# Seven-product weight sets for the merge gates, with a Mamba-2 (SSD) mixer cut into half groups beside them

## The chip, the core and the metric

The kernel runs on one core of a Trainium2 chip. TensorE (PE in the profile; PEld is its weight load) multiplies, VectorE (DVE), ScalarE (ACT) and GpSimd (POOL) do the elementwise work, and SyncE (SP) issues nearly all transfers. The metric is the time of one execution in device microseconds (us). Three runs of the kernel before took 1894.10, 1894.57 and 1894.77 us; the median is 1894.57 us.

## The reference

One decoder layer on 1024 tokens of width 1024, all in float32:

```
h  = RMSNorm(x);  P = h @ W_in                     # one projection, about 9250 columns
a  = RetNet retention (4 heads)                    -> 1024
b  = Mamba-2 SSD (16 heads of 64, 2 groups, state 128, chunks of 128 tokens) -> 1024
c  = gated linear attention (4 heads)              -> 1024
x  = x + (sig(g_a)*a + sig(g_b)*b + sig(g_c)*c) @ W_out
x  = x + relu(RMSNorm(x) @ W_up)^2 @ W_down;       final RMSNorm
```

The SSD part, for each chunk and head, with `a_cs` the running sum of the log decay inside the chunk:

```
l_mat  = exp(where(causal, a_cs[l] - a_cs[m], -inf))
y_diag = ((C B^T) * l_mat) @ xs                    # xs = x * dt
y_off  = (C @ state) * exp(a_cs)
state  = exp(a_cs[-1]) * state + B^T @ (xs * exp(a_cs[-1] - a_cs))
```

The three merge gates `sig(g + bias)` are 3072 columns of `P`: twelve sets of 256 columns.

## The kernel before

Float32 operands are split into a high and a low part by `split` (a cast on ACT, L156, and a subtraction on DVE, L157), and each product is three matmuls, high by high, high by low, low by high (`acc3`, L164). The input projection runs over 34 weight sets of 256 output columns. `projections` (L390 on) runs them one after the other: it fetches the raw weights two sets ahead, and `prep` makes the parts of the next set while `run_set` multiplies the current one.

A set has one of two forms. A "plain" set is four output tiles of 24 matmuls of 512 columns each, so 96. A "block" set takes the 2 by 2 blocks of weights and activations and forms the four output tiles from seven block products of 12 matmuls each (Strassen-Winograd), so 84; for that `prep` makes four more sums on DVE (L327 to L334) and the sums of the activations lie ready in `ht`. In a block set ACT copies the first product out of PSUM (L367), DVE adds it twice (`plus`, L361), and three of the four output tiles need one more DVE addition in the emitter (for the gates L487) ahead of the activation (L488). A set yields after each product (7 steps for a block set) or each output tile (4 steps for a plain set), and `merge` lays the steps of a mixer between these steps. The recording layer then sets each engine's order; the engines work through it strictly in that order.

Of the twelve gate sets, the first four are block sets and the last eight plain. The order of the stages is: 20 block sets, beside the first of them the rotary and the decay computations and the causal convolutions; four block sets beside the retention mixers; two block sets beside the log decays of GLA (`log_decays`); then `ht` is given up and the plain sets run beside `ssd_mixer(0)` and `ssd_mixer(1)` (26 steps), then the row statistics (`ssd_rows`), then the last five steps beside the first loads of the branch products.

`ssd_mixer(g)` works on a group of eight heads, chunk by chunk. `stage_a` loads the chunk (`xin`, and `ab`, the decay sums broadcast to all partitions), turns x and B by TensorE transposes (L705, L707), forms C B^T (L708), the scaled x (`xs`, `xd`), a copy of B (`bt`, ACT, L717), `eb` = exp of the decays (ACT, L725), and the decay mask in `ab`: a minimum with the row's own decay on DVE (L726), an exp with the negated decay as bias on ACT, one per head (L728), and a product with the masked C B^T on DVE (L729). `stage_b` multiplies (L741, L746, L750), adds up `y` and stores it; a sum of squares per row follows by a matmul against ones (L772). The exp of the mixer and the sigmoid of the gates are in different activation tables, so an ACT_TABLE_LOAD stands at each change between them.

At the start, `v_unit` multiplies the first 256 value columns together with the 32 columns of the SSD step sizes and the GLA gate (`w_vdg`), whose weights come in two pieces of 1152 columns (L961).

Of the kernel before, what the change touches and what calls it, by code (L numbers as in the profile page):

```python
# [51 lines left out]
def _layout(inp):  # L52
# [3 lines left out]
    a["w_vdg"] = vdg.reshape(2, 4, P, 288).transpose(0, 2, 1, 3).reshape(2, P, 1152)  # L56
# [55 lines left out]
def block_kernel(ctx, tc, i, out):  # L112
# [101 lines left out]
    ssq = ac.tile([P, 2 * NT], F32, name="ssq")  # L214
# [5 lines left out]
    nacs = ac.tile([P, NT, SH], F32, name="nacs")  # L220
# [66 lines left out]
    def v_unit(c, hc, p, ws):  # L287
        width = (288, 256)[p]
        ps = pmm.tile([P, 512], F32, name="mm", tag="mm")
        pairs = []  # L290
        for k in range(KD):
            hi, lo = ws[k // 4]
            o = (k % 4) * width
            pairs.append((hc[k], (hi[:, o:o + width], lo[:, o:o + width])))
# [200 lines left out]
    def decays():  # L495
# [32 lines left out]
        V.tensor_scalar(out=nacs, in0=acs, scalar1=-1.0, scalar2=None, op0=ALU.mult)  # L528
# [159 lines left out]
    def ssd_mixer(g):  # L688
        R = SH // SG
        hs = slice(g * R, (g + 1) * R)  # L690
        st = {"s": None}
        live = {}
# [3 lines left out]

        def stage_a(c):
            xin = sp.tile([P, 10, P], F32, name="xin", bufs=3)
            nc.sync.dma_start(out=xin, in_=st_d[g][c])
            ab = sp.tile([P, R, P], F32, name="ab", bufs=2)  # L700
            r0 = c * SH + g * R
            nc.sync.dma_start(out=ab, in_=acs_d[r0:r0 + R, :].partition_broadcast(P))
# [6 lines left out]
            ptv = pt.rearrange("p (h d) -> p h d", h=R)  # L709
            xs = sp.tile([P, R, SP], F32, name="xs", tag="w2m", bufs=11)  # L710
            V.tensor_tensor(out=xs, in0=ptv, in1=hb(dt, c), op=ALU.mult)
            xd = bt = eb = None
            if c + 1 < NT:
                xd = sp.tile([P, R, SP], F32, name="xd", tag="w2m", bufs=11)
                V.tensor_tensor(out=xd, in0=ptv, in1=hb(dtd, c), op=ALU.mult)
                bt = sp.tile([P, P], F32, name="bt", bufs=2)
                S.copy(out=bt, in_=bc[:, 0:128])  # L717
            cbm = sp.tile([P, P], F32, name="cbm", bufs=2)
            V.tensor_tensor(out=cbm, in0=bc[:, 128:256], in1=tri, op=ALU.mult)
            if c > 0:  # L720
                eb = sp.tile([P, 4, P], F32, name="eb", tag="w2m", bufs=11)
# [10 lines left out]
        def stage_b(c):  # L732
            xin, ab, xs, xd, bt, eb = live.pop(c)
            state = st["s"]
            y = sp.tile([P, 4, P], F32, name="y", tag="w2m", bufs=11)
            G.tensor_tensor(out=y, in0=xin[:, 0:4, :],
                            in1=d_c[:, 4 * g:4 * g + 4].unsqueeze(2).broadcast_to([P, 4, P]), op=ALU.mult)
# [5 lines left out]
            if c > 0:  # L743
                yo = pmx.tile([P, 4, P], F32, name="mx", tag="mx")
                for k in range(4):
                    PE.matmul(out=yo[:, k, :], lhsT=state[:, 2 * k:2 * k + 2, :].rearrange("p h d -> p (h d)"),  # L746
                              rhs=xin[:, 5, :], start=True, stop=True)
            if c + 1 < NT:
                sp_ = pmx.tile([P, 512], F32, name="mx", tag="mx")
                PE.matmul(out=sp_, lhsT=bt, rhs=xd.rearrange("p h d -> p (h d)"), start=True, stop=True)  # L750
                new = sp.tile([P, R, SP], F32, name="sst", tag="sst", bufs=2)
                nf = new.rearrange("p h d -> p (h d)")
                if c == 0:
                    V.tensor_copy(out=nf, in_=sp_)
                else:
                    G.tensor_tensor(out=new, in0=state, in1=hb(cdec, c), op=ALU.mult)
                    V.tensor_tensor(out=nf, in0=nf, in1=sp_, op=ALU.add)
                st["s"] = new
            V.tensor_tensor(out=y, in0=yd, in1=y, op=ALU.add)
            if c > 0:  # L760
                V.tensor_tensor(out=eb, in0=yo, in1=eb, op=ALU.mult)
                V.tensor_tensor(out=y, in0=y, in1=eb, op=ALU.add)
            V.tensor_tensor(out=y, in0=y, in1=xin[:, 6:10, :], op=ALU.mult)
            nc.sync.dma_start(out=o_d[2 + g][c // 4][:, :, c % 4, :], in_=y)
            sq = sp.tile([P, 4, P], F32, name="ysq", tag="w2m", bufs=11)
            S.activation(out=sq, in_=y, func=AF.Square)
            G.tensor_tensor(out=sq[:, 0:2], in0=sq[:, 0:2], in1=sq[:, 2:4], op=ALU.add)
            G.tensor_tensor(out=sq[:, 0], in0=sq[:, 0], in1=sq[:, 1], op=ALU.add)

            def stat():  # L770
                ps = ptp.tile([P, 512], F32, name="tp", tag="tp")
                PE.matmul(out=ps[:, 0:1], lhsT=sq[:, 0], rhs=ones[:, 0:1], start=True, stop=True)  # L772
                V.tensor_copy(out=ssq[:, g * NT + c:g * NT + c + 1], in_=ps[:, 0:1])
            return stat

        pend = []
        stage_a(0)
# [10 lines left out]
        yield  # L788
# [3 lines left out]
    def ssd_rows():  # L792
        r = rstd(wk, ssq, SH // SG * SP, 2 * NT)
# [132 lines left out]
    for g in range(SG):  # L926
        n = SET_S + 5 * g
        ssd.append([(n, e_conv(g, [(8 + g, 4), (10 + g, 5)]))])
        for m in range(2):
            ssd[g].append((n + 1 + 2 * m, e_plain(st_d[g], 6 + 2 * m, AF.Silu)))  # L930
            ssd[g].append((n + 2 + 2 * m, e_conv(g, [(4 * g + 2 * m, 2 * m), (4 * g + 2 * m + 1, 2 * m + 1)])))
    for n, (slot, func) in enumerate(((0, None), (2, None), (6, AF.Silu), (8, AF.Silu), (10, None), (12, None))):
# [3 lines left out]
            gla[3], ssd[1][4], gla[4], gla[5]]  # L936
    jobs = [("block", *j) for j in jobs]
    jobs += [("block" if n < 4 else "plain", SET_M + n, e_gate(n // 4, 2 * (n % 4))) for n in range(12)]
# [20 lines left out]
    def v_raw(name, q, n):  # L959
# [409 lines left out]
```

## Time and profile before

| what | value |
|---|---|
| median of three runs | 1894.57 us |
| the profiled execution | 1895.59 us, its span 1893.8 us |
| granted TensorE clock over the span | 0.995 |
| PE busy | 1863.7 us, 98% |
| DVE busy | 1129.8 us, 60% |
| ACT busy | 817.6 us, 43% |
| POOL busy | 204.6 us, 11% |
| chain that ended last | PE 34%, of it the line of all split matmuls, L164, 34% |

The stretches of the span, by the lines that run in them: block sets alone from 285 to 484 us, the retention mixers from 484 to 566 us, the log decays from 587 us, the SSD mixers beside plain sets from 643 to 836 us, GLA beside the branch products from 880 to 1000 us, after that output projection and MLP. Busy times of a matmul group overlap their neighbours, so the pace of TensorE is read from the count of matmuls in a stretch, not from the mean time of one.

### The profile page before, as it was taken

The numbers are of one execution on the slowest core, as the hardware profiler recorded it, in microseconds if no ns is written. First come the engines' busy times: TensorE is split into PE (matmuls) and PEld (weight loads), VectorE is DVE, ScalarE is ACT, GpSimd is POOL, SyncE is SP. The second block draws the span as 40 slices with busy tenths as digits, with TensorE's granted clock in tenths as the row PEclk, the third lists the DMA queues.
The fourth block names the chain that finished last, engine by engine and source line by source line (L and its number), as shares of the span: only waits on it lengthen the run. The fifth ranks groups of instructions, "written<-read, shape, count | busy, mean of one in ns | idle before, by whom it ended". The sixth has DMA issues, their size and how long they took to land. (4 is left out here: it accounts for less than half of the span.)

```text
span 1893.8 us, 25031 instructions
## 1 busy us (share of the span) xinstructions
PE 1863.7 (98%) x9372; PEld 1540.5 (81%) x9372; DVE 1129.8 (60%) x1707; ACT 817.6 (43%) x1432; POOL 204.6 (11%) x219
## 2 busy tenths in 40 slices
PE   8999999999999999999999999999999999999998
PEld 8977778888887777787878889988888888888886
DVE  6867766667555486746687467575545434444444
ACT  7522333334455687845663123454544421112213
POOL 1011100000220132321231030000000000000003
PEclk9999999999999999999999999999999999999999
DMA  6434434332753665547468454532323363322322
GB/s 215 149 112 145 134 98 128 97 111 90 222 151 117 236 210 175 179 123 262 154 211 300 147 153 157 200 134 98 125 94 120 124 218 103 97 89 89 98 70 89
DMA packets 174329, 275.89 MB, mean 146 GB/s; under 512 B 12384, under 2 KB 113792, under 8 KB 167552
## 3 DMA queue, kind: packets, MB, share of 16 engines
q1 hardware_dynamic: 173632, 273.38, 44.8%
q8 instruction: 74, 1.21, 0.3%
q10 hardware_dynamic: 576, 0.92, 0.2%
q14 instruction: 47, 0.39, 0.1%
HBM read 191.33 MB, written 78.72 MB: 143 GB/s over the span
## 5 line engine op out<-in xcount | busy, mean ns | idle before, releaser
L156 ACT CAST whi<-raw 128x1024 fp32r<-128x1024 f32 (+1 forms) x223 | 233.8, 1050 | 514.2 <-PE mm L164 484.8
L157 DVE TENSOR_TENSOR wlo<-raw,whi 128x1024 fp32r<-128x1024 f32 (+1 forms) x223 | 288.1, 1293 | 138.7 <-ACT whi L156 131.7
L164 PE MATMUL mm<-ht,whi 128*128 128x512 f32 x936 | 295.5, 397 | 2.2 <-DVE us L361 2.2
L164 PE MATMUL mm<-he,whi 128*128 128x512 f32 x672 | 214.2, 399 | 1.2 <-ACT us L367 0.9
L164 PEld LDWEIGHTS mm<-ht,whi 128*128 128x128 f32 x936 | 174.3, 188 | 46.9 <-DVE us L361 4.0
L164 PE MATMUL mm<-whi,al 128*128 128x512 f32 x512 | 202.5, 396 | 0.0
L164 PE MATMUL mm<-whi,ah 128*128 128x512 f32 x512 | 202.5, 395 | 0.0
L164 PE MATMUL mm<-wlo,ah 128*128 128x512 f32 x512 | 202.5, 395 | 0.0
L164 PE MATMUL mm<-ht,wlo 128*128 128x512 f32 x468 | 184.8, 395 | 0.0
L1313 DVE TENSOR_TENSOR x<-mm,x 128x512 f32<-128x512 f32 x128 | 88.3, 690 | 158.7 <-PE mm L164 158.7
L164 PEld LDWEIGHTS mm<-he,whi 128*128 128x128 f32 x672 | 124.7, 188 | 32.2 <-issue 1.7
L164 PE MATMUL mm<-hb,whi 128*128 128x512 f32 x464 | 149.2, 401 | 0.5 <-DMA hb<-b 0.5
L164 PE MATMUL mm<-he,wlo 128*128 128x512 f32 x336 | 133.5, 397 | 0.0
L164 PE MATMUL mm<-ht,w 128*128 128x512 f32 x468 | 116.1, 396 | 0.0
L164 PEld LDWEIGHTS mm<-whi,ah 128*128 128x128 f32 x512 | 96.2, 188 | 23.4
L164 PEld LDWEIGHTS mm<-whi,al 128*128 128x128 f32 x512 | 96.2, 188 | 23.3
L164 PEld LDWEIGHTS mm<-wlo,ah 128*128 128x128 f32 x512 | 96.2, 188 | 23.2
L361 DVE TENSOR_TENSOR us<-mm,us 128x512 f32<-128x512 f32 x78 | 53.8, 689 | 88.1 <-PE mm L164 86.5
L164 PEld LDWEIGHTS mm<-ht,wlo 128*128 128x128 f32 x468 | 87.7, 187 | 21.5
L164 PEld LDWEIGHTS mm<-ht,w 128*128 128x128 f32 x468 | 87.5, 188 | 20.9
L164 PEld LDWEIGHTS mm<-hb,whi 128*128 128x128 f32 x464 | 85.9, 188 | 22.2 <-issue 1.4
L164 PE MATMUL mm<-ohi,whi 128*128 128x512 f32 x256 | 103.1, 403 | 0.4 <-DVE gt L1097 0.4
(282 smaller groups left out, 3507.4 us busy)
## 6 DMA issues: line engine op xcount, KB each, us to landing
raw<-w_in SPq DMA_DIRECT2D x34, 1024.0 KB, 5.1
raw<-w_o SPq DMA_DIRECT2D x32, 512.0 KB, 4.0
raw<-w_up SPq DMA_DIRECT2D x16, 1024.0 KB, 5.0
act<-rl SPq DMA_DIRECT2D x64, 256.0 KB, 2.0
raw<-w_down SPq DMA_DIRECT2D x32, 512.0 KB, 4.3
araw<-act SPq DMA_DIRECT2D x64, 256.0 KB, 3.5
gate<-gt SPq DMA_DIRECT2D x48, 256.0 KB, 2.9
gt<-gate SPq DMA_DIRECT2D x48, 256.0 KB, 4.6
```

The source lines that it names most:

```text
L156: S.copy(out=dst_hi, in_=src)
L157: V.tensor_tensor(out=dst_lo, in0=src, in1=dst_hi.bitcast(F32), op=ALU.subtract)
L164: PE.matmul(out=ps, lhsT=l, rhs=r, start=(first and j == 0), stop=(last and j == n - 1), skip_group_check=open_)
L361: V.tensor_tensor(out=t, in0=ps, in1=other, op=ALU.add)
L1313: V.tensor_tensor(out=xs, in0=ps, in1=xs, op=ALU.add)
```

## The change

Eleven gate sets are block sets; one stays plain. The SSD mixers move ahead, beside nine block sets (`run(9)`, 63 steps), the log decays follow beside one (`run(1)`), then come the release of `ht` and the one plain set. `ssd_mixer(g, f4)` works on four heads, so there are four of them with eight chunks each: the tiles are half as large, the transposition of B, C B^T and the row statistic are done for each half group. The B transposition and C B^T now go into the PSUM tile of the x transposes (pool `ptp`, two tiles) and not into one of their own, and `y_off` into the tile of `y_diag`. The decay mask is made without the DVE minimum: per head a Relu on ACT, `relu(a_cs[l] - ab)`, then one Exp over all four heads with scale -1. Inputs of the next chunk are loaded one chunk ahead. The pool `up` has three buffers instead of four. `w_vdg` comes in pieces of 864, 864 and 576 columns, the third into tiles of its own. Two projection sets change place.

```diff
-    jobs += [("block" if n < 4 else "plain", SET_M + n, e_gate(n // 4, 2 * (n % 4))) for n in range(12)]
+    jobs += [("block" if n < 11 else "plain", SET_M + n, e_gate(n // 4, 2 * (n % 4))) for n in range(12)]
...
-    def ssd_mixer(g):
-        R = SH // SG
+    def ssd_mixer(g, f4):
+        R = SH // SG // 2
...
+        def load_in(c):
+            xin = sp.tile([P, 6, P], F32, name="xin", bufs=3)
+            nc.sync.dma_start(out=xin, in_=st_d[g][c][:, 4 * f4:4 * f4 + 6])
+            ab = sp.tile([P, R, P], F32, name="ab", bufs=3)
+            nc.sync.dma_start(out=ab, in_=acs_d[c * SH + h0:c * SH + h0 + R, :].partition_broadcast(P))
...
-            for j in range(4):
-                PE.transpose(out=pt[:, j * P:(j + 1) * P], in_=xin[:, j, :], identity=ident)
-            bc = pmx.tile([P, 512], F32, name="mx", tag="mx")
-            PE.transpose(out=bc[:, 0:128], in_=xin[:, 4, :], identity=ident)
-            PE.matmul(out=bc[:, 128:256], lhsT=xin[:, 4, :], rhs=xin[:, 5, :], start=True, stop=True)
+            for j in range(2):
+                PE.transpose(out=pt[:, j * P:(j + 1) * P], in_=xin[:, sx + j, :], identity=ident)
+            PE.transpose(out=pt[:, 256:384], in_=xin[:, sb, :], identity=ident)
+            PE.matmul(out=pt[:, 384:512], lhsT=xin[:, sb, :], rhs=xin[:, sb + 1, :], start=True, stop=True)
...
-            V.tensor_tensor(out=ab, in0=ab, in1=acs[:, c, hs].unsqueeze(2).broadcast_to([P, R, P]), op=ALU.min)
             for h in range(R):
-                S.activation(out=ab[:, h, :], in_=ab[:, h, :], func=AF.Exp, bias=nacs[:, c, g * R + h:g * R + h + 1])
+                S.activation(out=ab[:, h, :], in_=ab[:, h, :], func=AF.Relu, scale=-1.0,
+                             bias=acs[:, c, h0 + h:h0 + h + 1])
+            S.activation(out=ab, in_=ab, func=AF.Exp, scale=-1.0)
...
-    merge(run(2), 14, log_decays(ld), 9)
...
-    merge(itertools.islice(main, 26), 26, itertools.chain(ssd_mixer(0), ssd_mixer(1)), 38)
+    merge(run(9), 63, itertools.chain(*(ssd_mixer(g, f4) for g in range(SG) for f4 in range(2))), 72)
+    merge(run(1), 7, zip_steps(log_decays(ld), tail), 9)
...
-    merge(main, 5, itertools.islice(parts, 6), 6)
+    merge(main, 4, itertools.islice(parts, 6), 6)
```

The order on ACT in the middle of the SSD stage. Before, beside plain sets (`gt` is the gate's sigmoid, `eb` and `ab` the mixer's exps, `ysq` the square of y, `whi` the cast of the next weights):

```order
L725 ACT_TABLE_LOAD
L725 ACTIVATE eb<-ab 64x512 x2
L728 ACTIVATE ab<-ab,nacs 128x128 x8
L766 ACTIVATE ysq<-y 128x512
L488 ACT_TABLE_LOAD
L488 ACTIVATE gt<-mm,k_cols 128x512
L725 ACT_TABLE_LOAD
L725 ACTIVATE eb<-ab 64x512 x2
L488 ACT_TABLE_LOAD
L488 ACTIVATE gt<-mm,k_cols 128x512
L728 ACT_TABLE_LOAD
L728 ACTIVATE ab<-ab,nacs 128x128 x8
```

After, beside block sets, for one chunk of a half group (`bt` is the copy of B, the Relu is L734, the Exp over four heads L736):

```order
L487 ACT_TABLE_LOAD
L487 ACTIVATE gt<-gt,k_cols 128x512
L732 ACT_TABLE_LOAD
L732 ACTIVATE eb<-ab 64x256
L724 COPY bt<-tp 128x128
L732 ACTIVATE eb<-ab 64x256
L734 ACTIVATE ab<-ab,acs 128x128 x4
L487 ACT_TABLE_LOAD
L487 ACTIVATE gt<-gt,k_cols 128x512
L736 ACT_TABLE_LOAD
L736 ACTIVATE ab<-ab 128x512
L774 ACTIVATE ysq<-y 128x256
```

The chunk is half as large and has as many table loads about it. In the whole stage there are 38 loads before and 58 after.

The order on PE around one chunk's products. Before:

```order
L741 MATMUL mx<-ab,xs 64x128 x8
L746 MATMUL mx<-xin,sst 128x128 x4
L750 MATMUL mx<-xd,bt 128x512
L772 MATMUL tp<-ones,ysq 128x1
L705 MATMUL tp<-k_c_id,xin 128x128 x4
L707 MATMUL mx<-k_c_id,xin 128x128
L708 MATMUL mx<-xin 128x128
L164 MATMUL mm<-hb_5390,whi 128x512
```

After, up to the matmuls of the block set that stand between the products and the next transposes:

```order
L750 MATMUL mx<-ab,xs 64x128 x4
L754 MATMUL mx<-xin,sst 128x128 x2
L758 MATMUL mx<-xd,bt 128x256
L164 MATMUL mm<-ht_198,wlo 128x512
L779 MATMUL tp<-ones,ysq 128x1
L164 MATMUL mm<-hb_193,whi 128x512
```

Each half group has its own row statistic and, later on, its own transposition of B. Over the whole program the matmuls of 512 columns on the split line go from 6444 to 6360.

The order on ACT at the start of the program. Before (`he` is the high part of the first activations, which the first products need):

```order
L156 CAST whi<-raw 128x1152 x2
L240 ACTIVATE xr<-xr,rsx 128x1024
L235 ACTIVATE xsq,ssx<-xr 128x1024
L156 CAST he_191<-xe 128x8x128
L240 ACTIVATE xr<-xr,rsx 128x1024
```

After:

```order
L156 CAST whi<-raw 128x864 x2
L239 ACTIVATE xr<-xr,rsx 128x1024
L234 ACTIVATE xsq,ssx<-xr 128x1024
L156 CAST wv_270<-raw 128x576
L156 CAST he_191<-xe 128x8x128
```

The cast of the third weight piece now stands ahead of the cast of the activations.

## Rows read from the trace of the kernel before

**Rows 1.** The page's busy times of the engines over the span.

```profile
PE 1863.7 (98%) x9372; PEld 1540.5 (81%) x9372; DVE 1129.8 (60%) x1707; ACT 817.6 (43%) x1432; POOL 204.6 (11%) x219
```

**Rows 2.** Stretches: length; PE, PEld, DVE, ACT, POOL busy (instructions); clock; DMA share, GB/s.

```profile
285.00:484.00 199.00, 199.00 (x855) 159.95 (x854) 138.41 (x170) 76.96 (x90) 0.00 (x0) 1.00 0.36 109
643.00:836.00 193.00, 191.90 (x1108) 152.07 (x1107) 130.79 (x181) 145.58 (x260) 64.02 (x61) 1.00 0.56 175
880.00:1000.00 120.00, 112.35 (x639) 94.98 (x638) 93.46 (x278) 78.22 (x280) 34.00 (x40) 0.99 0.59 194
```

**Rows 3.** A stretch inside the SSD stage, columns as in Rows 2.

```profile
645.00:720.00 75.00, 74.06 (x439) 57.94 (x438) 56.27 (x80) 66.46 (x120) 26.07 (x25) 1.00 0.65 203
```

**Rows 4.** Groups on PE, 643 to 836 us: line, names, shapes, count | busy us, mean ns.

```profile
L164 PE MATMUL mm<-he,whi 128*128 128x512 f32 x190 | 61.9, 406 | 0.0
L164 PE MATMUL mm<-hb,whi 128*128 128x512 f32 x187 | 61.5, 407 | 0.0
L164 PE MATMUL mm<-he,wlo 128*128 128x512 f32 x96 | 38.7, 403 | 0.0
L164 PE MATMUL mm<-hb,wlo 128*128 128x512 f32 x95 | 37.7, 396 | 0.0
```

**Rows 5.** PE in order of time: start us, us, line, count of records merged.

```profile
708.34 0.28 PE L772 MATMUL tp<-ones,ysq 128*128 128x1 f32 x2
708.48 0.63 PE L705 MATMUL tp<-k_c_id,xin 128*128 128x128 f32 x4
708.95 0.27 PE L707 MATMUL mx<-k_c_id,xin 128*128 128x128 f32 x1
709.06 0.39 PE L708 MATMUL mx<-xin 128*128 128x128 f32 x2
709.20 0.48 PE L164 MATMUL mm<-hb,whi 128*128 128x512 f32 x1
```

**Rows 6.** Table loads on ACT, 643.4 to 838 us, columns as in Rows 4.

```profile
L488 ACT ACT_TABLE_LOAD x19 | 24.4, 1283 | 0.3
L725 ACT ACT_TABLE_LOAD x12 | 15.4, 1283 | 0.2
L728 ACT ACT_TABLE_LOAD x7 | 9.0, 1283 | 0.1
```

**Rows 7.** ACT in order of time: start us, us, count; in brackets the wait before.

```profile
700.62 1.28 ACT L488 ACT_TABLE_LOAD   x1
701.91 0.69 ACT L488 ACTIVATE gt<-mm,k_cols 128x512 f32<-128x512 f32 x1
702.50 0.26 ACT L717 COPY bt<-mx 128x128 f32<-128x128 f32 x1
702.77 1.28 ACT L725 ACT_TABLE_LOAD   x1
704.07 1.27 ACT L725 ACTIVATE eb<-ab 64x512 f32<-64x512 f32 x2
707.47 2.45 ACT L728 ACTIVATE ab<-ab,nacs 128x128 f32<-128x128 f32 x8 [2.13 <-DVE ab L726]
```

**Rows 8.** A group on ACT, 285 to 484 us (block sets), columns as in Rows 4.

```profile
L156 ACT CAST whi<-raw 128x1024 fp32r<-128x1024 f32 x31 | 32.5, 1050 | 72.9 <-PE mm L164 56.5 <-issue 10.6 <-DVE craw L452 5.4
```

**Rows 9.** A group on ACT, 587 to 643 us (log decays).

```profile
L566 ACT ACTIVATE az<-az 128x512 f32<-128x512 f32 x4 | 2.4, 629 | 0.0
```

**Rows 10.** Groups on DVE, 285 to 484 us (block sets).

```profile
L157 DVE TENSOR_TENSOR wlo<-raw,whi 128x1024 fp32r<-128x1024 f32 x31 | 37.8, 1223 | 17.6 <-ACT whi L156 17.6
L361 DVE TENSOR_TENSOR us<-mm,us 128x512 f32<-128x512 f32 x20 | 13.8, 689 | 15.3 <-PE mm L164 15.3
```

**Rows 11.** A group on DVE, 484 to 567 us (retention mixers).

```profile
L627 DVE TENSOR_TENSOR sm<-mx,dm 128x256 f32<-128x256 f32 x15 | 6.3, 418 | 0.8 <-PE mx L625 0.8
```

**Rows 12.** ACT at the start of the span, columns as in Rows 7.

```profile
12.10 1.04 ACT L156 CAST he<-xe 128x1024 fp32r<-128x1024 f32 x1 [1.03 <-DVE xe L249]
```

**Rows 13.** The page's DMA issues: KB each, median us from issue to landing.

```profile
gate<-gt SPq DMA_DIRECT2D x48, 256.0 KB, 2.9
```

More of the change, by code (lines that the diff above doesn't have):

```diff
@@ L213, in block_kernel @@
     dgt = ac.tile([P, NT, 32], F32, name="dgt")
-    ssq = ac.tile([P, 2 * NT], F32, name="ssq")
+    ssq = ac.tile([P, 2, 2 * NT], F32, name="ssq")
     rows = ac.tile([P, 32], F32, name="rows")
@@ L287, in v_unit @@
     def v_unit(c, hc, p, ws):
-        width = (288, 256)[p]
+        width, per = (288, 3) if p == 0 else (256, 4)
         ps = pmm.tile([P, 512], F32, name="mm", tag="mm")
@@ L291, in v_unit @@
         for k in range(KD):
-            hi, lo = ws[k // 4]
-            o = (k % 4) * width
+            hi, lo = ws[k // per]
+            o = (k % per) * width
             pairs.append((hc[k], (hi[:, o:o + width], lo[:, o:o + width])))
@@ L713, in stage_a @@
             if c + 1 < NT:
-                xd = sp.tile([P, R, SP], F32, name="xd", tag="w2m", bufs=11)
+                xd = w1m("xd", [P, R, SP])
                 V.tensor_tensor(out=xd, in0=ptv, in1=hb(dtd, c), op=ALU.mult)
                 bt = sp.tile([P, P], F32, name="bt", bufs=2)
-                S.copy(out=bt, in_=bc[:, 0:128])
+                S.copy(out=bt, in_=pt[:, 256:384])
             cbm = sp.tile([P, P], F32, name="cbm", bufs=2)
-            V.tensor_tensor(out=cbm, in0=bc[:, 128:256], in1=tri, op=ALU.mult)
+            V.tensor_tensor(out=cbm, in0=pt[:, 384:512], in1=tri, op=ALU.mult)
             if c > 0:
-                eb = sp.tile([P, 4, P], F32, name="eb", tag="w2m", bufs=11)
+                eb = w1m("eb", [P, 2, P])
                 av = ab.rearrange("p (k f) t -> p f k t", f=2)
@@ L734, in stage_b @@
             state = st["s"]
-            y = sp.tile([P, 4, P], F32, name="y", tag="w2m", bufs=11)
-            G.tensor_tensor(out=y, in0=xin[:, 0:4, :],
-                            in1=d_c[:, 4 * g:4 * g + 4].unsqueeze(2).broadcast_to([P, 4, P]), op=ALU.mult)
+            y = w1m("y", [P, 2, P])
+            k0 = 4 * g + 2 * f4
+            G.tensor_tensor(out=y, in0=xin[:, sx:sx + 2, :],
+                            in1=d_c[:, k0:k0 + 2].unsqueeze(2).broadcast_to([P, 2, P]), op=ALU.mult)
             yd = pmx.tile([P, 4, P], F32, name="mx", tag="mx")
@@ L743, in stage_b @@
             if c > 0:
[L744 to L747, printed above, removed]
+                for k in range(2):
+                    PE.matmul(out=yd[:, 2 + k, :], lhsT=state[:, 2 * k:2 * k + 2, :].rearrange("p h d -> p (h d)"),
+                              rhs=xin[:, sb + 1, :], start=True, stop=True)
             if c + 1 < NT:
                 sp_ = pmx.tile([P, 512], F32, name="mx", tag="mx")
-                PE.matmul(out=sp_, lhsT=bt, rhs=xd.rearrange("p h d -> p (h d)"), start=True, stop=True)
+                PE.matmul(out=sp_[:, 0:256], lhsT=bt, rhs=xd.rearrange("p h d -> p (h d)"), start=True, stop=True)
                 new = sp.tile([P, R, SP], F32, name="sst", tag="sst", bufs=2)
@@ L772, in stat @@
                 PE.matmul(out=ps[:, 0:1], lhsT=sq[:, 0], rhs=ones[:, 0:1], start=True, stop=True)
[L773 removed]
+                V.tensor_copy(out=ssq[:, f4, g * NT + c:g * NT + c + 1], in_=ps[:, 0:1])
             return stat
         pend = []
+        load_in(0)
+        yield
         stage_a(0)
@@ L792, in ssd_rows @@
     def ssd_rows():
-        r = rstd(wk, ssq, SH // SG * SP, 2 * NT)
+        V.tensor_tensor(out=ssq[:, 0], in0=ssq[:, 0], in1=ssq[:, 1], op=ALU.add)
+        r = rstd(wk, ssq[:, 0], SH // SG * SP, 2 * NT)
         yield
@@ L958, in block_kernel, with v_raw @@
         PE.matmul(out=wz[:, 0:128], lhsT=ones, rhs=ones, start=True, stop=True)
-    def v_raw(name, q, n):
-        raw = wp.tile([P, n], F32, name="raw", tag="raw", bufs=2)
-        nc.sync.dma_start(out=raw, in_=i[name][q])
+    def v_raw(k0, k1):
+        raw = wp.tile([P, 288 * (k1 - k0)], F32, name="raw", tag="raw", bufs=2)
+        nc.sync.dma_start(out=raw, in_=i["w_vdg"][:, 288 * k0:288 * k1])
         return raw
     rows_in = {0: x_load(0)}
-    raw0 = [v_raw("w_vdg", q, 1152) for q in range(2)]
+    raw0 = [v_raw(0, 3), v_raw(3, 6)]
     rows_in[1] = x_load(1)
     xn = {0: x_rows(rows_in.pop(0))}
-    w0 = [wparts(None, raw, 1152) for raw in raw0]
+    w0 = [wparts(None, raw, 864) for raw in raw0]
+    w0.append([pro.tile([P, 576], F32R, name=f"wv{q}", bufs=1) for q in range(2)])
+    split(*w0[2], v_raw(6, 8))
     hc = {0: x_chunk(0, xn.pop(0))}
@@ L1019, in block_kernel @@
     cvp = cst.enter_context(tc.tile_pool(name="cvp", bufs=2))
-    for _ in run(12):
+    for _ in run(11):
         pass
```

60 lines of the change are left out of this document (29 added, 31 removed).

## The prediction

> **What bounds the kernel now.** I read the page's busy shares first: PE is busy for 98% of the span, DVE for 60%, ACT for 43% [rows 1]. So a matmul saved is time saved wherever PE does not start to wait. Then the stretches: in the block sets alone 855 matmul records fill 199.00 us, and PE is busy for all of it [rows 2], which gives the pace, 199.00 / 855 = 0.2327 us for one matmul of 512 columns. In the SSD stage PE is still busy for 191.90 of 193 us, but ACT is at 145.58 us, 75%, and DVE at 130.79 us, 68% [rows 2]. The one thing to see here is that ACT is far busier beside the SSD mixers than beside block sets (77 of 199 us), and the change lays both on top of each other. So the sum has two parts: what PE saves, and whether ACT and DVE still keep up.
>
> **PE's work.** Seven sets go from 96 to 84 matmuls: 84 fewer, 84 x 0.2327 = 19.5 us less. The half groups add some: the transposition of B, C B^T and the row statistic are now done 32 times, not 16. From start to start one statistic takes 0.14 us (708.34 to 708.48), one transposition 0.11 (708.95 to 709.06) and one C B^T 0.14 (708.95 + 0.11 to 709.20) [rows 5]; 16 x 0.39 = 6.2 us. The x transposes, the products with `ab` and the state keep their number. The product of B and `xd` is cut from one of 512 columns into two of 256; the stream is the same and the start of one more instruction pair is bounded by 0 and by the 0.14 of the statistic, which streams one column; 14 more, 0 to 2 us, I take 0.8, in the middle. Together 7.0 us more. PE alone: -19.5 + 7.0 = -12.5 us.
>
> **The new SSD stage, engine by engine.** PE: of the 1108 records of the old stage 190 + 187 + 96 + 95 = 568 are set matmuls [rows 4], 568 x 0.2327 = 132.2 us, so the mixers cost 193 - 132.2 = 60.8 us, the waits of that stage included. The new stage is nine block sets, 9 x 84 x 0.2327 = 175.9, plus 60.8 + 7.0: 243.7 us.
>
> ACT, counted in the new order between the first mask and the last square: 58 table loads at 1.283 us [rows 6], 74.4; 128 Relus at 2.45 / 8 = 0.306 [rows 7], 39.2 (the price of the exps they replace, which have a bias column too); 32 Exps over four heads of 512 elements at 0.629 [rows 9], 20.1; 56 `eb` and 32 squares of 256 elements. For that width ACT has no row that I use; it lies between the 0.306 of 128 and the 0.629 of 512 elements, I take 0.40, a third of the way as the width is, 35.2. Then 36 sigmoids at 0.69 and 28 copies of B at 0.26 [rows 7], 24.8 and 7.3; 27 weight casts at 1.05 [rows 8], 28.4; and 18 casts and copies of 512 elements priced as the Exp, 11.3. Sum 240.7 us. With 256-wide work at its ends it is 232 to 261.
>
> DVE: 208 operations of 256 elements at 0.418 [rows 11], 86.9; 122 of 512 elements at 0.689 and 27 subtractions of 1024 at 1.223 [rows 10], 84.1 and 33.0; 64 narrow ones that cost less than the 256-wide, taken at half of it, 13. Sum 217 us, 89% of 243.7.
>
> So in this stage PE wants 243.7, ACT 240.7 and DVE 217 us. What the rectifier does is in these sums: without it DVE would have 32 minima of 512 elements more (22 us, 239), ACT 32 Exps less (221).
>
> **What the queues do with that.** ACT goes through its list in order and PE's product with `ab` waits for ACT's Exp and then DVE's product with C B^T. New is one more tie: the transposes of x share a tile with B, and a tile comes free only when ACT has copied B. The `tp` pool has two tiles, taken in turn by a chunk's transposes and a statistic, so in steady state the transposes of chunk c + 1 wait for ACT's copy of chunk c. Behind a transposition that waits stand PE's matmuls of the gate set. ACT's load is uneven: the order gives the sixth of the nine sets nine table loads and five chunks, the fifth one load and two chunks. Pricing each set as above, ACT exceeds PE by 0.5, 3.5, 3.7 and 3.5 us in four of them and falls short by up to 9.2 in the others. If nothing carries over, PE loses the sum of these, 11 us; if the excess carries over from set to set, its highest level is 4.8 us after the fourth set, and that much, less than a chunk of PE (243.7 / 32 = 7.6 us), can lie in the three `ab` buffers, so 0 at the other end. The nearest row is the old stage itself: in 645 to 720 us ACT is busy for 66.46 of 75 us, 89%, and PE still for 74.06 [rows 3], a loss of 1.3%. A loss of 2% of 243.7 is 5 us, and I take that.
>
> The log decays now run beside one block set, not two. Their 12 activations and some seven loads, with the set's own work, come by the prices above to about 25 us on ACT against some 24 on PE; 0 to 4 us, I take 1.
>
> **The start.** The first casts are smaller (864 columns, not 1152) and the first weights land sooner, but a third cast of 576 columns stands ahead of the cast of the activations, which starts at 12.10 us after its 1.03 us wait for DVE [rows 12], and which PE's first products await. Its piece (295 KB) is issued when DVE has split the first piece, by my working near 8.0 us; a transfer of 256 KB takes 2.9 us to land [rows 13], so about 11.2, the cast is done at 11.9, and nothing is lost. With 5 us to land 1.6 us would be; with all early, 0.3 gained. I take 0. The three `up` buffers hold the three sums of one set, and the first of the next set reuses one read two steps earlier: nothing, and if DVE lags by two steps (5 us) this is inside the wait already counted. The mixers' loads: SP issues a chunk's inputs a chunk ahead, some 7 us against the 2.9 us of such a transfer; covered.
>
> **Sum.** -19.5 + 7.0 + 5 + 1 = -6.5 us. The profiled execution took 1895.59 us, so 1889.1; the median of the runs is 1.0 us under the profiled one: 1888 us.
>
> **A page against it.** ACT's sequence of a sigmoid, a load and an exp shows a load of 1.28 us, begun at 702.77 as the copy ended (702.50 + 0.26), and the exp at 704.07, 0.02 us after it [rows 7]. The Trainium skill, ScalarE: Activation LUTs, "What ACT_TABLE_LOAD costs", states 1283 ns for the load and a further drain of 1380 ns for every switch of set. By that rule 58 switches would add 80 us to ACT. The trace agrees on the load and shows no drain.
>
> **The rivals.**
> - *ACT sets the pace, slower.* PE and ACT wait for each other by turns: PE for the mask and for the copy of B, ACT for sums that DVE makes of PE's products. With ACT's 240.7 us and the stage's gain gone at 243.7 + 12.5 = 256 us, it decides from ACT being busy for less than 94% of the stage. At 90 to 92% the stage takes 262 to 267 us, and the time is 1901 to 1906, with the log decays. For it: in the old stage ACT waited 2.13 us for DVE in the middle of a chunk [rows 7], and in the GLA stage, a chain of the same kind, PE is busy for only 112.35 of 120 us with ACT at 65% [rows 2]. Against it: the row of 645 to 720 us. Chance 0.22.
> - *No change.* DVE's 217 us is priced from rows without much POOL work; with DVE's operations a tenth dearer it is as full as the other two, and PE loses some 5% of the stage, 12 us: 1895. Chance 0.21.
> - *All of PE's saving arrives.* The excess of ACT lies in the buffers and the 1.3% of waits that the mixers' 60.8 us holds goes too: 1895.6 - 12.5 - 1.0 = 1882, or 1880 if those waits vanish. For it: PE's waits in the old stage are 1.1 us. Chance 0.18.
> - *A switch costs more than its load*: if ACT stands still for as long again, 58 x 1.283 = 74 us, it needs 315 us, 71 over PE's 243.7, and the time is 1882 + 71 = 1953. In the old stage the exp followed its load at once [rows 7]; chance 0.01. (The Trainium skill's drain, above, is this rival.)
>
> The forecast, 3 to 7 us lost to waits and 1886 to 1891 us, has 0.38. **Chances and range.** What can be told from no change is 0.2%, 3.8 us: faster is under 1890.8, slower over 1898.4. Forecast and full saving, 0.56 together, lie under that but for a little, so faster 0.54; no change with that little 0.22; the ACT rival and the dearer switch, with a little from the dearer DVE, 0.24. The range reaches from the full saving with its waits, 1879, to 1903, inside the ACT rival at 91.5%; it leaves out a tenth at the top and about as much below.
>
> **What would show it.** The stage of the four half mixers: nine sets in 245 to 252 us, PE busy for over 96% of it, ACT for over 93%, DVE near 88%. 6360 matmuls of 512 columns on the split line, all stages behind the SSD stage the same length as before. The rival on ACT is right if the products with `ab` or the transposes of x show waits of more than 12 us in all, behind DVE's `ab` and ACT's copy of B. The sum is wrong at PE if a half group's chunk costs more than 2.1 us of PE; the price of the half-width ACT work is wrong if 256-wide `eb` takes 0.5 us or more. The start is wrong if the first product starts later than 13.2 us by more than 0.5.

## The result and the profile after

The changed kernel takes 1909.39 us (median of 6, 1908.64 to 1912.21) against 1894.46 us (1893.47 to 1895.33): ratio 1.0082 [1.0069, 1.0095]. It is slower by 15 us; the forecast was 1888 with a range from 1879 to 1903, so the prediction was wrong. The profiled execution has a span of 1907.6 us, 13.8 more than before.

The page's busy times after, to be laid beside [rows 1]:

```profile
PE 1866.1 (98%) x9396; PEld 1538.6 (81%) x9396; DVE 1175.6 (62%) x1921; ACT 892.7 (47%) x1568; POOL 199.9 (10%) x247
```

PE still looks full, so the page doesn't show the loss. The starts of single instructions do (start us, us, engine and line): the first product of the retention mixers and the first branch product (`ohi`). Before:

```profile
485.28 0.64 PE L625 MATMUL mx<-rin 128*128 128x128 f32 x4
868.51 0.39 PE L164 MATMUL mm<-ohi,whi 128*128 128x512 f32 x1
```

After:

```profile
466.37 0.60 PE L623 MATMUL mx<-rin 128*128 128x128 f32 x4
882.29 0.39 PE L164 MATMUL mm<-ohi,whi 128*128 128x512 f32 x1
```

So the first product of the retention mixers begins at 466.4 us, before at 485.3: 18.9 us gained. One block set has moved from the part ahead of it into the middle part, where fourteen block sets and one plain stand in place of six and eight; that is why the 84 matmuls are missing ahead (1758 recorded before, 1674 after) while the middle part has 1194 in both. From there to the first branch product it takes 415.9 us, before 383.2: 32.7 lost. From there to the end it is 1025.3 us in both. The SSD stage lies in the middle part. Stretches of the changed kernel, columns as in [rows 2], the whole stage and two pieces of it:

```profile
568.00:838.00 270.00, 259.50 (x1413) 204.32 (x1413) 195.13 (x416) 232.27 (x414) 55.88 (x88) 0.98 0.54 160
633.00:636.00 3.00, 2.81 (x14) 2.38 (x15) 1.78 (x5) 1.69 (x5) 0.00 (x0) 0.50 0.46 153
695.00:700.00 5.00, 4.64 (x18) 3.74 (x19) 3.13 (x7) 4.95 (x12) 0.00 (x0) 0.50 0.38 112
```

The stage takes 270 us, not 245 to 252. ACT is busy for 232.27 us of it, 86%, less than the 93% that I asked for. In the two short pieces the granted clock is 0.50, the lower level of 1.2 GHz, where the rows of the old SSD stage have 1.00 [rows 2, 3]. What PE waited for in the old stage (643 to 836 us; total us, times, longest):

```profile
PE mx L741 <- DVE ab L729: 0.9, 2, 0.7
PE tp L772 <- DVE ssq L773: 0.2, 1, 0.2
```

And in the new one:

```profile
PE tp L779 <- POOL ysq L775: 5.2, 3, 2.6
PE tp L713 <- DMA xin<-st: 1.5, 3, 1.2
PE tp L713 <- DVE cbm L726: 1.5, 1, 1.5
PE mx L750 <- DVE ab L737: 1.4, 4, 0.5
PE tp L713 <- DMA ab<-acs_d: 0.8, 1, 0.8
```

The largest wait is at the row statistic (L779), for which the prediction had no wait. In order of time at the longest one (start us, us, engine and line; in brackets the wait before):

```profile
628.55 0.60 PE L758 MATMUL mx<-xd,bt 128*128 128x256 f32 x2
628.80 0.58 PE L164 MATMUL mm<-ht,wlo 128*128 128x512 f32 x1
...
628.82 0.42 DVE L767 TENSOR_TENSOR y<-mx,y 128x256 f32<-128x256 f32 x1 [1.71 <-PE mx L754]
630.43 0.43 DVE L771 TENSOR_TENSOR y<-y,xin 128x256 f32<-128x256 f32 x1
...
629.21 1.28 ACT L734 ACTIVATE ab<-ab,acs 128x128 f32<-128x128 f32 x4
630.95 0.42 ACT L774 ACTIVATE ysq<-y 128x256 f32<-128x256 f32 x1 [0.46 <-DVE y L771]
...
631.45 0.45 POOL L775 TENSOR_TENSOR ysq<-ysq 128x128 f32<-128x128 f32 x1 [4.58 <-ACT ysq L774]
...
631.96 0.38 PE L779 MATMUL tp<-ones,ysq 128*128 128x1 f32 x2 [2.57 <-POOL ysq L775]
```

Between this chunk's last product and its statistic PE's list holds a single matmul of the block set, and the way over DVE, ACT and POOL takes 3.2 us. PE stands for 2.57 us, and at 632.8 the clock falls.

The whole middle part, from the first retention product to the first branch product, worked out from the starts of PE's records: a set matmul counts 0.2327 us and what its interval to the next start has above that is "over pace"; the intervals of the small products are a row of their own; idle time is taken out of both; the rest is what half-clock stretches add. The 26 small products that run in such stretches count in their own row with 2.6 us, their price in c3. The three right columns are runs told below.

| us | before | after | before, tanh (c4) | after, tanh (c3) | c3's code, after's order (e1) |
|---|---|---|---|---|---|
| 1194 recorded set matmuls | 277.8 | 277.8 | 277.8 | 277.8 | 277.8 |
| over pace | 10.6 | 16.2 | 9.9 | 14.3 | 16.4 |
| small products of the mixers | 90.3 | 101.4 | 90.4 | 101.6 | 100.8 |
| idle | 4.4 | 13.4 | 3.3 | 4.5 | 13.3 |
| half clock (rest) | 0.1 | 7.1 | 0.0 | 0.1 | 5.5 |
| sum | 383.2 | 415.9 | 381.4 | 398.3 | 413.8 |

So 32.7 = 5.6 + 11.1 + 9.0 + 7.0: 16.7 us of PE's own work, and 16.0 of waits and half clock.

### The profile page after: what moved, and what is told of

Same layout as the page of the kernel before. It is cut to its first block, busy times and chain, and to the rows that moved or that the text cites. A ratio compares the mean times of both kernels' runs of the same rounds, so it can differ in the third digit from the quotient of the medians.

```text
span 1907.6 us, 25681 instructions
## 1 busy us (share of the span) xinstructions
PE 1866.1 (98%) x9396; PEld 1538.6 (81%) x9396; DVE 1175.6 (62%) x1921; ACT 892.7 (47%) x1568; POOL 199.9 (10%) x247
## 5 line engine op out<-in xcount | busy, mean ns | idle before, releaser
L164 PE MATMUL mm<-ht,whi 128*128 128x512 f32 x1104 | 353.9, 401 | 2.5 <-DVE us L360 2.5
L164 PEld LDWEIGHTS mm<-ht,whi 128*128 128x128 f32 x1104 | 206.0, 189 | 52.8 <-DVE us L360 4.2
L164 PE MATMUL mm<-ht,wlo 128*128 128x512 f32 x552 | 219.7, 399 | 0.0
L164 PE MATMUL mm<-he,whi 128*128 128x512 f32 x560 | 182.7, 404 | 0.2
L164 PE MATMUL mm<-ht,w 128*128 128x512 f32 x552 | 138.2, 397 | 0.0
L164 PEld LDWEIGHTS mm<-ht,wlo 128*128 128x128 f32 x552 | 104.1, 189 | 25.0
L164 PEld LDWEIGHTS mm<-he,whi 128*128 128x128 f32 x560 | 104.9, 190 | 23.9 <-ACT us L366 0.3
L360 DVE TENSOR_TENSOR us<-mm,us 128x512 f32<-128x512 f32 x92 | 63.4, 689 | 90.7 <-PE mm L164 90.4
L164 PE MATMUL mm<-he,wlo 128*128 128x512 f32 x280 | 111.8, 399 | 0.0
L164 PE MATMUL mm<-ohi,wlo 128*128 128x512 f32 x256 | 102.0, 398 | 0.0
L164 PE MATMUL mm<-olo,whi 128*128 128x512 f32 x256 | 102.0, 398 | 0.0
```

The source lines that it names most:

```text
L164: PE.matmul(out=ps, lhsT=l, rhs=r, start=(first and j == 0), stop=(last and j == n - 1), skip_group_check=open_)
L360: V.tensor_tensor(out=t, in0=ps, in1=other, op=ALU.add)
```

## The experiments

**First theory: places and ACT's load.** Four kernels, timed against 1892.77 us. The step (a `yield`, at which `merge` lets matmuls of the sets in between) that used to stand ahead of a mixer's last two statistics comes back:

```diff
+        yield
         for stat in pend:
             stat()
```

> The changed kernel, with the step put back that the change took out ahead of the last two row statistics of each mixer (76 mixer steps, not 72). Theory S (PE stands at a statistic that is asked for right behind the chunk's own products, since its square and its POOL sum come late, and then runs at half clock): the three waits for POOL's sum of 2.9, 1.0 and 2.0 us and most of the half clock in the stage (10.2 us, half of it lost) go, 1897 to 1901 us. Theory A (ACT sets the pace of the stage): the waits only move to the next thing that ACT makes, 1906 to 1910 us.

1912.72 us, 1.0103 [1.0085, 1.0121]. The wait stayed, for the recording layer set the statistic right behind the products again. PE's largest wait in the stage of this run:

```profile
PE tp L779 <- POOL ysq L775: 6.8, 4, 3.9
```

The mask again by DVE's minimum and one exp per head:

```diff
-                S.activation(out=ab[:, h, :], in_=ab[:, h, :], func=AF.Relu, scale=-1.0, ...)
-            S.activation(out=ab, in_=ab, func=AF.Exp, scale=-1.0)
+            V.tensor_tensor(out=ab, in0=ab, in1=acs[...].broadcast_to([P, R, P]), op=ALU.min)
+                S.activation(out=ab[:, h, :], in_=ab[:, h, :], func=AF.Exp, bias=nacs[...])
```

> The changed kernel with the decay mask as before, a minimum on DVE and one exp per head with the negated decay as bias; half groups and block sets stay. Takes 32 Exps of 0.63 us, 20 us, from ACT and gives DVE 32 minima of 0.69 us, 22 us. Theory A (ACT sets the pace): 1895 to 1902 us. Theory S (the statistic's place): 1905 to 1911 us. Theory D (DVE is the late one): 1915 us or more.

1908.33 us, 1.0078 [1.0061, 1.0096]: without the rectifier the loss is as large, so it isn't the cause by itself. In the trace the middle part is 4.8 us shorter than in the changed kernel (411.1) and the part behind it 4.1 longer.

The gates by Exp, so that ACT's table need not be switched (11 loads, not 76). This kernel leaves out the sigmoid, so its output isn't the layer's; it serves to time the loads:

```diff
-            S.activation(..., func=AF.Sigmoid, bias=mb_c[...])
+            S.activation(..., func=AF.Exp, bias=mb_c[...])
```

> The changed kernel with Exp in place of Sigmoid in the twelve gate sets, so that the gates are the exp of their argument; the table loads between gates and mixers go (76 loads in the program become 11, 83 us of ACT), nothing else moves. Theory A (ACT with its loads sets the pace): 1885 us or less. Theory S: the square and the sum are a little earlier, 1900 to 1906 us, and the waits for the statistic stay above 3 us. If neither: 1909 us.

1900.83 us, 1.004 [1.0025, 1.0056]. The SSD stage is 20 us shorter (250) and without a wait for the statistic, but behind it PE waits 6.4 us for the `hb` loads.

Half groups and the rectifier beside plain sets, at the place that the mixers had before:

```diff
-    jobs += [("block" if n < 11 else "plain", ...) for n in range(12)]
+    jobs += [("block" if n < 4 else "plain", ...) for n in range(12)]
```

> The half-group mixers with the rectifier, beside plain sets as in the kernel before (four block sets and eight plain ones among the gates). Against the kernel before this adds PE's 7 us of doubled transposes, C B^T and statistics, and no block set. If half groups cost only that: 1901 to 1903 us. Theory S says more, since the flush of the statistics is in it: 1904 to 1910 us. If the trouble is only block sets with mixers beside them: 1898 to 1902 us.

1917.42 us, 1.0132 [1.0113, 1.015]: beside plain sets, too, the half-group mixers lose, 25 us; the changed kernel with its block sets is 8 us faster than that.

**Second: statistics and tables apart, and on both kernels.** Four kernels, against 1893.19 us. The statistics asked for four chunks later:

```diff
+            stats.append(nxt)
+            if len(stats) > 4:
+                stats.pop(0)()
```

> The changed kernel with each row statistic asked for four chunks later, also across the four half mixers (the POOL sum goes into a tile of its own; the square's tile comes from another pool). Theory S (PE waits for the statistic's sum, then runs at half clock): the 5.3 us of waits behind POOL and the two half-clock stretches behind them (10.2 us, 5 lost) go: 1898 to 1902 us. Theory A (ACT with its table loads is the limit of the stage): the waits come back at the product with the mask, 1905 to 1911 us.

1905.0 us, 1.0066 [1.0046, 1.0086]. The whole time hides a part of the effect: the middle part is 9.7 us shorter than in the changed kernel (406.2), but the part behind it 7.2 longer, with 19.2 us at half clock in place of 3.7. The statistic's waits are gone, and others stand in their place, the largest of them:

```profile
PE mm L164 <- ACT us L366: 3.5, 2, 2.1
```

The gates as half of one plus tanh of half the argument, which computes the same and shares exp's table:

```diff
+    mbh = const.tile([P, 24], F32, name="mbh")
+    V.tensor_scalar(out=mbh, in0=mb_c, scalar1=0.5, scalar2=None, op0=ALU.mult)
...
-            S.activation(..., func=AF.Sigmoid, bias=mb_c[...])
+            S.activation(..., func=AF.Tanh, scale=0.5, bias=mbh[...])
...
-            V.tensor_tensor(out=gt, in0=ps, in1=gt, op=ALU.mult)
+            V.scalar_tensor_tensor(out=gt, in0=gt, scalar=1.0, in1=ps, op0=ALU.add, op1=ALU.mult)
...
-                split(m[0], m[1], accs[d])
+                S.activation(out=m[0], in_=accs[d], func=AF.Copy, scale=0.5)
+                V.scalar_tensor_tensor(out=m[1], in0=accs[d], scalar=0.5, in1=m[0].bitcast(F32), ...)
```

> The changed kernel with the gates as 0.5 (1 + tanh(x/2)): the 1 and the 0.5 ride on instructions that are there already (the product with the branch, the split of the merged sum), so the only thing that goes is 65 of 76 table loads, 83 us of ACT. Theory A: as the run with Exp gates, 1898 to 1902 us; the stage of the half mixers near 250 us. If that run was fast for another reason: 1906 to 1910.

1880.37 us, 0.9933 [0.9916, 0.995]: faster than both kernels, and by more than any theory had said. With the statistics deferred as well:

> Both: late statistics and tanh gates. If the two are separate causes, their gains add: 1888 to 1894 us. If they are one cause (ACT late, and the statistic only the place where PE feels it): no better than tanh gates alone, 1898 to 1902 us.

1883.69 us, 0.9947 [0.9929, 0.9966]: no further gain. The same gates in the kernel before:

> The kernel before with tanh gates, nothing else: 41 of 52 table loads go. There ACT was busy for 75% of the SSD stage and PE waited 1 us in it, so 1890 to 1894 us, within 0.25% of the kernel before. Much less would say that table loads cost PE time beside plain sets too, where no wait shows them.

1882.42 us, 0.9945 [0.9926, 0.9964], more than expected. The traces showed why: in the two tanh kernels the last stage, which no edit touches, was 6.8 us shorter.

**Third: the tile that came along.** Against 1893.89 us. Two kernels get only the tile `mbh`, two get tanh without it (the halved bias written over the bias).

> The kernel before with one tile more, 24 numbers in each partition, written once at the start and read by nobody; sigmoids and table loads stay as they are. In the two kernels with tanh gates the last stage (down) ran 1535 matmul records in 351.4 us, 0.2289 us each, and in all others in 358.2 us, 0.2333 each, though nothing in that stage was edited; both held this tile. Theory P (the tile shifts every tile behind it in SBUF, and the pace of a matmul hangs on where its operands lie): the last stage takes 351.4 us here too, and the kernel is 6 to 8 us faster than before, about 1886. Theory T (the gain of tanh comes from the table loads in every stage): no change, 1892 to 1895, and 358.2 us in the last stage.

> The changed kernel with the same idle tile of 24 numbers; 76 table loads as before the edit. Theory P: last stage 351.4 instead of 358.2 us and about 1902, with the SSD stage as long as in the changed kernel (265 to 272 us). Theory T: 1908 to 1911.

> The changed kernel with tanh gates, 11 table loads, but the halved bias is written over the bias, so that no tile is added and nothing shifts. Theory P: last stage 358.2 us, and 1886 to 1889, with the SSD stage at 250 us as with the tile. Theory T: 1879 to 1882 again, last stage 351.4 us.

> The kernel before with tanh gates, 11 table loads, the halved bias written over the bias, no tile added. Theory P: last stage 358.2 us, and 1888 to 1892, that is 2 to 6 us faster than before from the loads alone. Theory T: 1881 to 1884 again.

Measured, in that order: 1884.2 us, 0.9958 [0.9941, 0.9974]; 1904.06, 1.0054 [1.0039, 1.0069]; 1888.94, 0.9976 [0.9967, 0.9985]; 1890.2, 0.9982 [0.9973, 0.9991]. The idle tile gains what theory P said and more (9.7 us, and 5.3 against the changed kernel's 1909.39); without it tanh takes the changed kernel from 1909 to 1889. The stage of c3:

```profile
568.00:818.00 250.00, 248.16 (x1388) 198.23 (x1388) 197.19 (x415) 157.53 (x356) 58.45 (x87) 1.00 0.57 173
```

And PE's waits in that stage of c3:

```profile
PE tp L714 <- DMA xin<-st: 1.0, 2, 0.8
PE tp L714 <- DVE us L361: 0.8, 1, 0.8
```

250 us at a clock of 1.00, and next to no wait. (Of the 20 us to the changed kernel's stage 5 are no gain: 744 set matmuls fall into this stage, 766 into that one. The whole middle part is 17.6 us shorter.) That reads like proof that the table loads on ACT were the cause. But the recording layer sets a new order when the loads go: 963 of the 8832 places in PE's list hold another row (the expectation below counts 412 rows). The kernel with Exp gates had nearly the same new order.

**Fourth: the loads and the order apart.** Against 1894.45 us. Every engine's instructions are chained in a given order:

```diff
+        for a, b in zip(row, row[1:]):
+            tc.add_manual_dep(mine[b], mine[a].name, free, reason="order")
```

> Tanh gates written over the bias as before (13 table loads instead of 76, no tile added), but every engine's order is pinned to that of the changed kernel: PE, SP and POOL are row for row the same, ACT and DVE but for the loads and the gates' own instructions. In the run with tanh gates the recording layer, which counts table loads, had also set another order (412 rows of PE's list differ). Theory L (the loads' own time on ACT is the cause): 1887 to 1892, the SSD stage 249 to 254 us, no wait for the row statistic above 1 us. Theory O (the order that the layer makes for the loads is the cause, above all statistics asked for too early): 1903 to 1909, the stage 263 to 270 us, the waits of 2.6 and 1.8 us for the statistic still there.

> The changed kernel with its sigmoids, and every engine's order pinned to that of the run with tanh gates in place; on that order 63 table loads stand instead of 76. Theory L: ACT is as late as in the changed kernel, 1903 to 1912, the SSD stage 262 to 272 us. Theory O: the better order hides the loads, 1887 to 1893, stage 249 to 255 us. Both half: 1895 to 1902 in this run and in the other.

e1: 1907.46 us, 1.0072 [1.0055, 1.0088], hardly faster than the changed kernel. The same stretch of it (the stage ends at 836.4, 1.7 us earlier than in the changed kernel):

```profile
568.00:838.00 270.00, 260.72 (x1426) 205.75 (x1426) 196.20 (x419) 157.81 (x358) 57.86 (x89) 0.98 0.54 161
```

And PE's two largest waits in it:

```profile
PE tp L780 <- POOL ysq L776: 5.2, 3, 2.6
PE tp L714 <- DMA xin<-st: 2.1, 3, 1.2
```

ACT fell from 232.27 to 157.81 us, 58% of the stage, and PE waits at the same rows for about as long. So in this order it isn't ACT's table loads that PE waits for. e1 and c3 are the same code in two orders (13 loads and 11), and the order makes 18.5 us of difference. e2: 1933.3 us, 1.0208 [1.0192, 1.0223], beyond every forecast; on the better order the loads are dear. PE's largest wait in its stage is at the mask:

```profile
PE mx L750 <- DVE ab L737: 21.4, 6, 4.6
```

Both theories in their simple form fell: neither the loads' going nor the order alone gives the gain of c3.

**Fifth: which rows of the order.** Two pairs of kernels, against 1893.4 and 1893.9 us. First, in the changed kernel's own order, the two statistics that stand 1 and 5 set matmuls behind their products are moved (PE, once with sigmoids, once with tanh on the old order):

```diff
 MATMUL mx<-xd,bt 128x256
 MATMUL mm<-ht,wlo 128x512
-MATMUL tp<-ones,ysq 128x1
 MATMUL mm<-he,whi 128x512
 ...
-MATMUL tp<-ones,ysq 128x1
+MATMUL tp<-ones,ysq 128x1 x2
```

> The changed kernel, sigmoids and 76 loads as they are, with every engine's order pinned to its own and only two rows moved on PE: the row statistic of the seventh chunk of the first and of the second half group, which stood 1 and 5 set matmuls behind its products, stands in front of the next chunk's statistic, 20 and 29 behind; DVE's two copies of these sums move along. Theory O: the waits of 2.6 and 1.8 us go, and with them the half-clock stretches at 632.8 and 694.2 us (10.2 us at half clock), together 9 to 10 us: 1898 to 1901. Theory N (the place of two statistics is a symptom; the same time is then lost at the next products): 1905 to 1910.

> The same two rows moved in the run with tanh gates on the changed kernel's order (1907.5 us, no switches of the table in the stage). Theory O: 1896 to 1900. Theory N: 1903 to 1908. If this run and the one with sigmoids agree within 3 us, the table loads cost nothing in this order.

1908.71 us, 1.0084 [1.0067, 1.0101], and 1906.49, 1.0068 [1.0052, 1.0085]. The first also speaks against a cost of the chaining itself: it has the changed kernel's order but for these rows, and its time (1909.39). In the first of them PE now waits at the same two places for the copy of a block product, its largest wait:

```profile
PE mm L164 <- ACT us L366: 5.4, 2, 3.0
```

Then ACT's two copies are moved ahead as well:

```diff
+COPY us<-mm 128x512
 ACTIVATE ab<-ab,acs 128x128 x4
 ACTIVATE ysq<-y 128x256
 ACTIVATE ab<-ab 128x512
-COPY us<-mm 128x512
```

> The run with the two statistics moved, with sigmoids and 76 loads, and two rows more moved on ACT at the same two places: ACT's copy of a block product out of PSUM (`us`), which stood behind four Relus, a square and an Exp, now stands ahead of them. PE had waited 3.0 and 2.4 us for these copies at 633.0 and 692.7 us. Theory O (a few rows in the order of PE and ACT make the loss): both waits go, 5 us, and with them the half-clock stretch of 3.4 us at 693: 1900 to 1903. Theory N (PE's time at the end of a half group is bound by the chain from its products over DVE and ACT to the next ones, whichever row meets it first): 1905 to 1909, and the next products with `ab` or the next statistic wait instead.

> The same rows moved in the run with tanh gates on the changed kernel's order. Theory O: 1897 to 1901. Theory N: 1903 to 1907.

1909.03 us, 1.0084 [1.0061, 1.0107], and 1904.17, 1.0058 [1.0041, 1.0076]. In the run with sigmoids the wait has gone on to the next products:

```profile
PE mx L750 <- DVE ab L737: 5.8, 4, 2.8
```

Theory N held: whichever row comes first there waits out the chain. What the two orders differ in is how far apart the chunks' product groups (the four products with `ab` and those behind them) stand. Counted in PE's list, set matmuls between one group and the next over the first 16 half chunks (before: over its 16 chunks); the least is that of the whole list, and the middle part is the one from the first retention product to the first branch product:

| kernel | set matmuls from group to group | least | middle part, us | whole, us |
|---|---|---|---|---|
| before | 23 32 22 31 24 36 24 72 24 48 24 24 48 24 24 | 22 | 383.2 | 1894 |
| after | 24 31 18 23 28 31 **2** 35 29 18 24 27 29 **6** 23 | 2 | 415.9 | 1909 |
| a1, step restored | 18 27 28 15 37 31 **0** 36 29 18 24 27 29 **6** 11 | 0 | 419.1 | 1913 |
| a2, minimum on DVE | 24 30 21 29 23 29 **9** 39 28 22 15 12 43 10 31 | 9 | 411.1 | 1908 |
| b1, statistics deferred | 24 31 18 23 19 29 13 38 30 16 23 19 28 14 23 | 11 | 406.2 | 1905 |
| c3, tanh | 24 12 24 24 24 12 24 48 12 24 24 24 12 24 24 | 12 | 398.3 | 1889 |
| e2, c3's order with sigmoids | as c3 | 12 | 440.9 | 1933 |

In the changed kernel the longest waits stand where two groups are 2 and 6 matmuls apart (0.5 and 1.4 us of PE): the second group needs the mask and the states for which DVE and ACT have only just got the first group's results. In c3 no two groups are less than 12 apart. From a1 to c3 the middle part gets shorter as the least distance grows. That the distances are the cause is argued and not shown: no run changed them alone, c3 has no table loads in the stage, and e2 has c3's distances and is the slowest of all.

## Why the prediction was wrong

- **The steps that failed are two terms of the sum: the 6 us for waits (5 in the SSD stage, 1 at the log decays) and the 7.0 us for half groups on PE.** The runs show 16.0 and 16.7 in their place. With 18.9 saved, not 19.5, that makes -18.9 + 16.7 + 16.0 = 13.8 us where the sum had -6.5; each of the two misses is about half of the gap.
- **The waits.** I took them as a share of the stage from one row of the old order [rows 3], by ACT's busy share, and let the three `ab` buffers carry the unevenness. The runs show idle time up by 9.0 us and 7.0 more at half clock. The size hung on the order of the lists and not on how busy ACT is: with ACT at 58% (e1) the stage was nearly as long, and the same code in c3's order was 18.5 us faster. I had read in the order that one set holds five chunks and another two, and priced that on ACT as work to be done; on PE it meant two product groups side by side, with the chain between them, which no busy share shows. That this nearness makes the waits is the reading that fits the table above; it isn't shown by itself.
- **Half clock had no term.** It was 0.1 us before and 7.1 after. Stretches of 3.4 and 6.8 us begin 0.8 and 0.5 us after the waits of 2.57 and 1.83 us; c3, without these waits, has none in the stage. A third, of 6.8 us at 844.4 beside the log decays, follows a wait of only 0.67 us, and why it came is open.
- **The price of half groups on PE, 7.0 us, was less than half of the truth.** Small products and time over pace add 16.7 us, and 15.6 in c3 against c4, which waits don't disturb. The transposes, C B^T and the statistic come near their 6.2 (7.4 from c4 to c3). What I gave no price is that each group of products is entered and left twice as often. From start to start a product with `ab` takes 0.055 to 0.059 us in the mean inside a group, the last of a group 0.203, the set matmul ahead of one 0.325 instead of 0.233; from c4 to c3 products with `ab` went from 16.4 to 20.3 us though they are 256 in both, and the pace of the set matmuls lost 4.4. The sign named for this came out: c3's stage has 248.2 us of busy PE, 744 set matmuls take 173.1 of it, and the rest is 2.3 us for each of 32 chunks, over the 2.1.
- **The saving was right**: 18.9 us are gained by the first retention product, for 19.5. So were the prices on ACT. The groups in the stage, columns as in [rows 4]:

```profile
L734 ACT ACTIVATE ab<-ab,acs 128x128 f32<-128x128 f32 x128 | 41.1, 391 | 5.9 <-DMA ab<-acs_d 5.2
L487 ACT ACT_TABLE_LOAD x29 | 37.2, 1283 | 0.5
L732 ACT ACT_TABLE_LOAD x20 | 25.7, 1283 | 0.3
L732 ACT ACTIVATE eb<-ab 64x256 f32<-64x256 f32 x56 | 23.3, 415 | 0.9
L736 ACT ACT_TABLE_LOAD x9 | 11.5, 1283 | 0.2
```

  58 loads take 74.4 us as forecast, `eb` 0.415 us (0.40), and all of ACT 232 (240.7). DVE needed 195 (217).
- **The rival on ACT** gave the nearest time, 1901 to 1906, but not for its reason: its own sign, more than 12 us of waits at the products with `ab` and the transposes of x, isn't there (1.4 and 3.8 us), and e1 takes ACT away as the direct cause in this order. The loads count all the same: with them on the even order (e2) PE waits 21.4 us for the mask. The gain of c3 needs both, no loads and the order that the layer makes without them.
- **The drain** of the Trainium skill, ScalarE: Activation LUTs, "What ACT_TABLE_LOAD costs", 1380 ns beside the load, isn't in the trace after either: the exp stands 0.02 us behind its load (a load from 627.04 for 1.28 us, `eb` at 628.34).
- **Start and log decays**: the first product starts at 12.6 us (13.2 before), nothing lost. Between the stage and the first branch product PE waits 1.3 us, near the 1 us forecast; the half-clock stretch there is the third one above.
- **No gain even undisturbed**, as far as the tanh kernels show it: c3 and c4 differ by 1.3 us (1888.94 and 1890.2), and their intervals overlap. The 18.5 us saved up to the retention mixers are met by 16.9 up to the branch products, 15.6 of it PE's own work. That c3 lies near the forecast of 1888 is luck: its gain comes with the tanh gates, which make the kernel before 4 us faster as well.

What stays open: why the layer's order bunches the chunks, whether the bunching alone makes the waits, and whether an even order can be found that also hides 58 loads; it wasn't tried.

## What to carry to other kernels

Where a layer sets the order, look in the changed order for the least distance between dependent groups on the bottleneck engine, and price the chain between them by rows; busy shares say nothing of it. Halving a group's size doubles its entries and exits, even where the number of products stays, and that is work on PE which no wait shows. Compare variants by the part that the edit touches as well as by the whole time: b1 gained 9.7 us there and lost most of it elsewhere. An edit that takes away a stall may also change the order and the place of every tile: fix the order, and compare a stage that the edit doesn't touch, before the gain is put down to the stall.

## What the hardware showed unexpectedly

A tile of 24 numbers per partition that nobody reads made the last stage faster. PE's list is the same row for row with it and without (c1 and before, c2 and after). A stretch of that stage of 300 us, in the kernel before; in brackets behind PE the number of matmuls:

```profile
1560.00:1860.00 300.00, 300.00 (x1288) 241.50 (x1287) 136.65 (x190) 59.90 (x87) 6.46 (x5) 1.00 0.27 86
```

In c1, the kernel before with the tile:

```profile
1560.00:1860.00 300.00, 300.00 (x1312) 246.08 (x1311) 138.86 (x194) 62.58 (x95) 11.95 (x12) 1.00 0.27 84
```

And in c3, the changed kernel with tanh and without the tile:

```profile
1560.00:1860.00 300.00, 300.00 (x1287) 241.58 (x1286) 135.26 (x188) 59.70 (x88) 9.07 (x7) 1.00 0.26 83
```

One matmul takes 0.2289 us with the tile and 0.2333 without (351.4 and 358.2 us from the first to the last of 1536 records), at the same granted clock. That the tile moves all tiles behind it is the only difference but for the one DVE instruction that writes it at the start; which tile's place does it, and how, was not tried. It is worth 6.8 us, near half of the change's whole loss, and is part of the fastest version measured, the changed kernel with tanh gates and the tile (b2, 1880.37 us; the kernel before with both, b4, 1882.42).

Not every wait of PE brings the clock down: in c3 a wait of 2.54 us at 883.7 us was followed by no stretch at 1.2 GHz, nor was one of 3.03 us at 633.0 us in f1, while after the changed kernel's wait of 1.83 us the granted clock was 0.50 for 6.8 us.
